# Full-height and full-width stationary operands in the mixers of a two-block network

## The chip, the cores and the metric

One NeuronCore of a Trainium2 chip runs the whole program. The metric is device time in microseconds; three runs of the kernel before took 3250.97, 3258.43 and 3259.24 us, so the median is 3258.43 us.

## The reference, cut to what matters

The input is one sequence of 512 tokens of width 1024. The first block puts 16 meta tokens in front of them (528 positions) and runs two layers, each of a SwiGLU network, a mixer and a second SwiGLU network. The second block is one layer with another mixer and a SwiGLU network. All of it is float32.

A mixer of the first block adds up two branches:

```python
# attention: 8 heads, 96 features a head for scores, 64 for values
s = einsum('bhqd,bkhd->bhqk', q, k) * 96 ** -0.5     # causal over meta and tokens
o = einsum('bhqk,bkhd->bqhd', softmax(s), v)
# recurrence: 4 heads of 128 features, decay exp(b_t - b_s) for each pair t >= s
attn = einsum('bhtk,bhtsk,bhsk->bhts', q, decay, k)
o = einsum('bhts,bhsv->bhtv', attn, v) + (what the state brings)
```

The second block's mixer has a state-space branch, and an attention branch of 8 query heads over one shared key head of 64 features, where a query sees only the 128 keys with the highest index score:

```python
rel = relu(einsum('bqhd,bsd->bqhs', qi, ki))          # 4 index heads of 64 features
iscore = einsum('bqhs,bqh->bqs', rel, wi)             # top 128 visible keys are kept
logits = einsum('bqhd,bqkd->bhqk', q, kg) * 64 ** -0.5
```

## The kernel before, in words

Activations lie with features on the partitions and positions along the free dimension, in 74 slots of 128 x 528 floats that are handed out and taken back in rotation (`alloc`, `free`, lines 262 to 275). Weights come in 512 KB chunks through three buffers on SP's DMA queue; ScalarE (ACT) and GpSimd or VectorE (POOL, DVE) split each into a high and a low part, up to four chunks ahead of their use (`split`, `ahead`). A dense product is three TensorE (PE) instructions for each 128 x 128 piece of the weight: high by high, high by low, low by high (`dense`, line 678, in the mixers; lines 400 to 402 in the networks). A product of plain float32 operands stands in the trace as two instructions, a transpose as one.

`weave` merges lists of small items by their costs into one order, so that each mixer's attention, its recurrence and the dense products of the next group of heads alternate on PE, one instruction or a few at a time. Each engine then runs its own queue in a fixed order, and engines wait for each other through semaphores.

What the change touches:

* `attention` (from line 700) serves both blocks. `s_pass` makes the scores of one head and one query block of 128 (line 719) and the exponentials. `t_pass` turns the probabilities so that keys lie on partitions: `nb` transposes of 128 x 128 (line 743), and, in the first block, one of the odd 16 keys that are left over (line 747). In the first block the keys stand with the 16 meta keys first, so that the odd keys are the last 16 tokens of the query block; only its rows from 96 on see them, and the transpose is of 32 rows and 16 columns. `o_pass` multiplies by the values: line 768 for each block of 128 keys, line 771 for the odd keys, of 16 rows and 32 columns. With one block of keys (`nb == 1`), line 768 is used twice, for query rows 0 to 95 and 96 to 127.
* `mixer`: `values` (line 954) makes the value tiles by blocks of 128 positions from position 0, the last of 16; `att_items` says which of them a head reads; `take` (line 1165) makes the products of one level of the recurrence's decay, four chunks of 128 positions each (line 1187), and for the level of 64 the quarter of each chunk that is wanted, 64 columns by 64 (line 1184).
* `block_2`: `kk_norm` (line 1569) normalizes one tile that holds the index key on partitions 0 to 63 and the key on 64 to 127, and copies it with its halves exchanged. `score` (line 1591, 4 heads for each of 3 query blocks) and `att` (line 719, 8 heads for each of 4 query blocks) take 64 partitions of the tile that has the wanted key beside the wanted head.

In the first block a layer has 8 heads and 4 query blocks of tokens, so 64 units of attention over the two layers, 16 of them with `nb == 1`; layer 0 has 8 more units for the 16 meta queries (`nb == 0`). The recurrence has 4 heads a layer and 4 chunks a head.

Of the kernel before, what the change touches and what calls it, by code (L numbers as in the profile page):

```python
# [8 lines left out]
F32 = mybir.dt.float32  # L9
# [9 lines left out]
META = 16  # L19
L = SEQ + META  # L20
# [233 lines left out]
class Kernel:  # L254
# [448 lines left out]
    def attention(self, units, geom, q, k, bias, sc, values, put):  # L703

        nc = self.nc
        U = {}

        def width(u):
            _, _, nb, meta = geom(units[u][1])
            return 128 * nb + META * meta  # L710

        def s_pass(u):
            h, qt = units[u]
            c0, n, nb, meta = geom(qt)
            qa, ka = q(h)[:, c0:c0 + n], k(h)
            w = META * meta + 128 * nb
            w0 = min(w, 512)
            ps = self.bank()
            nc.tensor.matmul(ps[:n, :w0], qa, ka[:, :w0], start=True, stop=True)
            if w > w0:  # L720
                pm = self.bank()[:n, :w - w0]
                nc.tensor.matmul(pm, qa, ka[:, w0:w], start=True, stop=True)
            p = self.alloc("p")
            nm = self.small.tile([128, 1], F32, name="nm")
            sm = self.small.tile([128, 1], F32, name="sm")
            nc.vector.tensor_tensor_reduce(p[:n, :w0], ps[:n, :w0], bias(qt)[:, :w0], -sc, 3e38, OP.add, OP.min, nm[:n])
            if w > w0:
                n0, nm = nm, self.small.tile([128, 1], F32, name="nm2")
                nc.vector.tensor_tensor_reduce(p[:n, w0:w], pm, bias(qt)[:, w0:w], -sc, n0[:n], OP.add, OP.min, nm[:n])
            self.sc.activation(p[:n, :w], p[:n, :w], AF.Exp, scale=-1.0, bias=nm[:n], accum_out=sm[:n])  # L730
            ri = self.small.tile([128, 1], F32, name="ri")
            nc.vector.reciprocal(ri[:n], sm[:n])
            U[u] = (p, ri)

        def t_pass(u):
            h, qt = units[u]
            c0, n, nb, meta = geom(qt)
            p, ri = U[u]
            ps = self.bank()
            pt = self.alloc("pt") if nb else None  # L740
            ptm = self.meta_tile("ptm") if meta else None
            for b in range(nb):
                nc.tensor.transpose(ps[:, 128 * b:128 * b + n], p[:n, 128 * b:128 * b + 128], self.ident[:n, :n])
            if meta:
                r0 = 96 if nb else 0
                pm = (ps[:META, 128 * nb:128 * nb + n - r0] if nb < 4 else self.bank()[:META, :n - r0])
                nc.tensor.transpose(pm, p[r0:n, 128 * nb:128 * nb + META], self.ident[r0:n, r0:n])

            def cp(d, s):
                if u % 2 == 0:  # L750
                    nc.vector.tensor_copy(d, s)
                else:
                    self.sc.activation(d, s, AF.Copy)
            if nb:
                cp(pt[:, :128 * nb], ps[:, :128 * nb])
            if meta:
                cp(ptm[:, :n - r0], pm)
            self.free(p)
            U[u] = (pt, ptm, ri)

        def o_pass(u):

            h, qt = units[u]
            c0, n, nb, meta = geom(qt)
            at = {}

            def times_v(b, r0, r1, start, stop):
                nc.tensor.matmul(at["bk"][r0:r1], U[u][0][:, 128 * b + r0:128 * b + r1], values(b, h), start=start, stop=stop)

            def rest(r0, start, stop):  # L770
                nc.tensor.matmul(at["bk"][r0:], U[u][1][:, :n - r0], values(nb, h)[:META], start=start, stop=stop)
            if nb == 0:
                fns = [(rest, 0, True, True)]
            elif nb == 1 and meta:
                fns = [(times_v, 0, 0, 96, True, True), (times_v, 0, 96, n, True, False), (rest, 96, False, True)]
            else:
                fns = [(times_v, b, 0, n, b == 0, b == nb - 1) for b in range(nb)]
                if meta:
                    fns.insert(1, (rest, 96, False, False))

            def fn(i, f, *args):
                if i == 0:
                    at["bk"] = self.bank()[:n, :64]
                f(*args)
                if i == len(fns) - 1:
                    pt, ptm, ri = U.pop(u)
                    nc.vector.tensor_scalar(put(h, qt)[:n, 64 * (h % 2):64 * (h % 2) + 64], at["bk"], ri[:n], None, op0=OP.mult)
                    if pt is not None:
                        self.free(pt)
            return [Item((0.00088 * width(u) + 0.1) / len(fns), lambda i=i, f=f: fn(i, *f)) for i, f in enumerate(fns)]  # L790

        n = len(units)
        items = []
        for t in range(n + 2):
            if t < n:
                items.append(Item(0.0017 * width(t) + 0.1, lambda t=t: s_pass(t)))
            if 0 <= t - 1 < n:
                items.append(Item(0.00085 * width(t - 1) + 0.1, lambda t=t: t_pass(t - 1)))
            if 0 <= t - 2:
                items += o_pass(t - 2)  # L800
        return items
# [97 lines left out]
    def mixer(self, l, st, nxt):  # L899
# [57 lines left out]
        def values():  # L957
# [1 line left out]
            hi, lo = self.split_of[f"v{l}"]  # L959
            vs = []  # L960
            for b in range(5):
                c0, nt = 128 * b, min(128, L - 128 * b)
                bk = self.bank()[:nt, :512]
                for k in range(2):
                    for i, (x, w) in enumerate(((hs, hi), (ls, hi), (hs, lo))):
                        nc.tensor.matmul(bk, x[k][:, c0:c0 + nt], w[:, k, :], start=k == 0 and i == 0, stop=k == 1 and i == 2)
                t = self.alloc(f"v{b}")
                self.sc.activation(t[:nt, :512], bk, AF.Copy)
                vs.append(t)
            S["v"] = vs  # L970
# [34 lines left out]
        def att_items(j):  # L1005
# [4 lines left out]
                return self.mask[:, 384 - 128 * qt:L] if qt < 4 else self.mask[:META, META + 384:2 * META + 384]  # L1010

            def values(b, h):
                return S["v"][b][:128 if b < 4 else META, 64 * h:64 * h + 64]

            def put(h, qt):
                if ("o", j) not in S:
# [48 lines left out]
        def hg_items(j):  # L1065
# [98 lines left out]
            def take(i):  # L1164
# [9 lines left out]
                def product(c):  # L1174
# [5 lines left out]
                        at["ps"] = self.bank()  # L1180
                    ps, (lhs, rhs) = at["ps"], X["x", i]
                    sl = slice(128 * c, 128 * c + 128)
                    if h == 64:
                        nc.tensor.matmul(ps[:64, 64 * c:64 * c + 64], lhs[:, 128 * c:128 * c + 64],
                                         rhs[:, 128 * c + 64:128 * c + 128], start=True, stop=True)
                    else:
                        nc.tensor.matmul(ps[:, nq2 * c:nq2 * c + nq2], lhs[:, sl], second(rhs[:, sl]), start=True, stop=True)
                    if c == 3:
                        keep(ps, lhs, rhs)
                        X.pop(("x", i))  # L1190
# [356 lines left out]
    def block_2(self, st, nxt):  # L1547
# [20 lines left out]

        def kk_norm():
            head_norm("kk", "kk2")  # L1570
            k2 = S["kk_"] = self.alloc("kk_")
            self.sc.activation(k2[0:64, :n], S["kk"][64:128, :n], AF.Copy)
            self.sc.activation(k2[64:128, :n], S["kk"][0:64, :n], AF.Copy)

        def vw_turn():
            e = S.pop("vw")
# [8 lines left out]

        def score(qt, h):
            w = 128 * (qt + 1)
            row = slice(64 * (h % 2), 64 * (h % 2) + 64)
            ki = S["kk" if h % 2 == 0 else "kk_"]
            ps = self.bank()[:, :w]  # L1590
            nc.tensor.matmul(ps, S[f"qi.{h // 2}"][row, 128 * qt:128 * qt + 128], ki[row, :w], start=True, stop=True)
            rel = self.alloc("rel")
            self.sc.activation(rel[:, :w], ps, AF.Relu)
            if h == 0:
# [25 lines left out]

        def att(qt):
            def q(h):
                return S[f"q.{h // 2}"][64 * (h % 2):64 * (h % 2) + 64]

            def k(h):
                return S["kk" if h % 2 else "kk_"][64 * (h % 2):64 * (h % 2) + 64]
            return self.attention([(h, qt) for h in range(8)], lambda qt: (128 * qt, 128, qt + 1, False), q, k, bias, 64 ** -0.5,
                                  lambda b, h: S["vt"][:, 68 * b:68 * b + 64], put)

        def finish():  # L1630
            for j in range(4):
                o = S.pop(("o", j))
                S["ot", j] = self.o_turn(o, None, n)
                self.free(o)
            self.free(S.pop("kk"), S.pop("kk_"), S.pop("vt"), *[S.pop(f"qi.{m}") for m in range(2)],
                      *[S.pop(f"q.{m}") for m in range(4)], *[S.pop(("sc", qt)) for qt in (1, 2, 3)])
            self.split_y(S, "yb", "ot", n)

# [168 lines left out]
        for m in range(4):  # L1807
            c += glu(m)
        P += weave(q_items, [x for qt in (1, 2, 3) for x in scores(qt)],
                   [item(lambda: load_out(0)), item(lambda: states(0), 5.0), item(lambda: load_out(1)), item(lambda: states(1), 5.0)])  # L1810
        P += weave(gates[:6 * per], [item(residual)] + tops(1) + tops(2), inner(0) + inner(1) + inner(2) + inner(3), att(0))
        P += weave(gates[6 * per:12 * per], tops(3), att(1) + att(2), c)
        P += weave(att(3) + [item(finish, 1.0)], gates[12 * per:])
# [29 lines left out]
    def setup_late(self):  # L1843
# [9 lines left out]
        nc.sync.dma_start(self.reset, self.ins["reset"])  # L1853
        self.ident = const("ident", [128, 128])
        self.halves = const("halves", [128, 128])
        self.lmask = self.cst.tile([128, len(LEVELS) + 1, 128], U8, name="lmask")
        for i in range(2):
            t = self.alloc("lm")
# [95 lines left out]
```

## Time and profile before

| what | before |
|---|---|
| median of three runs | 3258.43 us |
| the profiled execution, its own time | 3261.48 us |
| its span, first to last instruction | 3259.7 us |
| PE busy | 3174.7 us (97%), 21610 instructions |
| PE weight loads busy | 2869.4 us (88%) |
| DVE busy | 2038.7 us (63%) |
| ACT busy | 1407.6 us (43%) |
| POOL busy | 1080.1 us (33%) |
| DMA | 28.2% of 16 engines, 88 GB/s |

PE's busy time is the union of its instructions' intervals, and these overlap: a dense product of 264 columns has a duration of some 0.28 us, while the next one ends 0.12 us after it. What an instruction takes of PE's time is therefore read from ends: the end (start plus duration) of the one before, its own end, and the end of the one after. The three mixers run at about 498 to 794 us, 1742 to 2033 us and 2566 to 2800 us of the span; the rest are the networks, projections and the ends.

### The profile page before, as it was taken

To read this page: it belongs to the slowest core of one execution; us is meant where nothing else is said; L and a number is where in the kernel's file an instruction comes from. 1 tells how busy PE (TensorE), PEld (TensorE's weight loads), DVE (VectorE), ACT (ScalarE), POOL (GpSimd) and SP (SyncE) were. 2 spreads that over 40 slices of the span, in tenths; PEclk is the share of its full clock that TensorE was granted. 3 is DMA by queue.
4 is the path that set the end of the run, shared out by engine and by line. 5 is a ranking of instruction groups with operands and counts; after the bars stand their busy time and mean duration, and the time that the engine had idled before them with its cause. 6 is when DMAs were issued, how large, how long until landed. Compare 5 with 4: busy or idle time off the path is not lost. (4 is left out here: it accounts for less than half of the span.)

```text
span 3259.7 us, 53075 instructions
## 1 busy us (share of the span) xinstructions
PE 3174.7 (97%) x21610; PEld 2869.4 (88%) x21610; DVE 2038.7 (63%) x3417; ACT 1407.6 (43%) x2385; POOL 1080.1 (33%) x656
## 2 busy tenths in 40 slices
PE   9999999999999999999999999999999889999999
PEld 9999998889999999999998777888988566788988
DVE  7564456663575755856665563576757785566664
ACT  5322344444343544534544443444546335444443
POOL 3453235443222122222234453322224533322122
PEclk9999999999999999999998999999999999999999
DMA  5333221111323233233231112223235331222232
GB/s 185 124 107 106 91 87 44 46 53 59 92 72 110 83 94 104 79 97 104 89 99 54 41 52 65 85 91 104 86 103 162 105 89 56 72 91 92 91 98 97
DMA packets 106532, 289.63 MB, mean 89 GB/s; under 512 B 23088, under 2 KB 32304, under 8 KB 106288
## 3 DMA queue, kind: packets, MB, share of 16 engines
q1 hardware_dynamic: 106288, 286.24, 28.2%
q8 instruction: 170, 2.79, 0.4%
q14 instruction: 74, 0.61, 0.1%
HBM read 272.96 MB, written 13.24 MB: 88 GB/s over the span
## 5 line engine op out<-in xcount | busy, mean ns | idle before, releaser
L317 POOL TENSOR_TENSOR wlo<-raw,whi 128x1024 fp32r<-128x1024 f32 (+3 forms) x320 | 713.7, 2232 | 1488.9 <-ACT whi L218 1427.6
L218 ACT ACTIVATE whi<-raw 128x1024 fp32r<-128x1024 f32 (+2 forms) x504 | 491.5, 979 | 873.7 <-PE bank L401 329.1
L401 PE MATMUL bank<-gl,whi 128*128 128x264 f32 (+1 forms) x1408 | 439.1, 312 | 0.0
L402 PE MATMUL bank<-gh,wlo 128*128 128x264 f32 (+1 forms) x1408 | 439.1, 312 | 0.0
L400 PE MATMUL bank<-gh,whi 128*128 128x264 f32 (+1 forms) x1408 | 438.9, 312 | 0.0
L678 PE MATMUL bank<-xh,whi 128*128 128x264 f32 (+2 forms) x1224 | 428.4, 350 | 0.0
L678 PE MATMUL bank<-xl,whi 128*128 128x264 f32 (+2 forms) x1224 | 423.8, 346 | 3.0 <-DVE xl L421 2.8
L678 PE MATMUL bank<-xh,wlo 128*128 128x264 f32 (+2 forms) x1224 | 419.8, 343 | 0.0
L400 PE MATMUL bank<-xh,whi 128*128 128x264 f32 (+1 forms) x1184 | 356.5, 302 | 5.5 <-DVE t L576 4.6
L401 PE MATMUL bank<-xl,whi 128*128 128x264 f32 (+1 forms) x1184 | 355.2, 301 | 2.7 <-DVE xl L421 2.5
L402 PE MATMUL bank<-xh,wlo 128*128 128x264 f32 (+1 forms) x1184 | 355.1, 301 | 1.3 <-POOL wlo L317 1.3
L317 DVE TENSOR_TENSOR wlo<-raw,whi 128x1024 fp32r<-128x1024 f32 (+1 forms) x184 | 231.4, 1257 | 80.6 <-ACT whi L218 80.3
L400 PEld LDWEIGHTS bank<-gh,whi 128*128 128x128 f32 x1408 | 264.8, 188 | 16.0 <-issue 0.4
L402 PEld LDWEIGHTS bank<-gh,wlo 128*128 128x128 f32 x1408 | 264.9, 188 | 15.8
L401 PEld LDWEIGHTS bank<-gl,whi 128*128 128x128 f32 x1408 | 264.7, 188 | 15.7
L678 PEld LDWEIGHTS bank<-xl,whi 128*128 128x128 f32 (+1 forms) x1224 | 234.2, 191 | 28.7 <-issue 6.4
L678 PEld LDWEIGHTS bank<-xh,whi 128*128 128x128 f32 (+1 forms) x1224 | 234.4, 191 | 25.4 <-issue 6.2
L678 PEld LDWEIGHTS bank<-xh,wlo 128*128 128x128 f32 (+1 forms) x1224 | 234.1, 191 | 25.0 <-issue 8.1
L635 DVE SCALAR_TENSOR_TENSOR h<-bank,h 128x264 f32<-128x264 f32 (+1 forms) x192 | 89.6, 496 | 236.3 <-PE bank L402 235.5
L400 PEld LDWEIGHTS bank<-xh,whi 128*128 128x128 f32 x1184 | 223.1, 189 | 14.3 <-DVE t L576 5.0
L218 ACT ACTIVATE whi<-s 128x512 fp32r<-128x512 f32 x272 | 162.8, 626 | 168.1 <-PE bank L521 98.5
L401 PEld LDWEIGHTS bank<-xl,whi 128*128 128x128 f32 x1184 | 223.6, 189 | 11.3 <-DVE xl L421 3.5
(428 smaller groups left out, 7879.9 us busy)
## 6 DMA issues: line engine op xcount, KB each, us to landing
raw<-in_w_dram SPq DMA_DIRECT2D x423, 512.0 KB, 3.5
raw<-in_w_dram SPq DMA_DIRECT2D x80, 448.0 KB, 3.3
h<-in_x_dram SPq DMA_DIRECT2D x8, 264.0 KB, 5.7
s_t<-zero SPq DMA_DIRECT2D x8, 256.0 KB, 5.5
s_wo<-cm SPq DMA_DIRECT2D x16, 128.0 KB, 3.2
s_win<-cm SPq DMA_DIRECT2D x8, 256.0 KB, 2.4
s<-s_win SPq DMA_DIRECT2D x8, 256.0 KB, 4.3
s<-s_wo SPq DMA_DIRECT2D x8, 256.0 KB, 3.7
```

The source lines that it names most:

```text
L218: i = self.e.activation(out, in_, func, **kw)
L317: e.tensor_tensor(lo[:, a:b], src, hi[:, a:b].bitcast(F32), op=OP.subtract)
L400: mm(p, hi[:, wk, :m], xh[k][:, c0:c1], start=start, stop=False)
L401: mm(p, hi[:, wk, :m], xl[k][:, c0:c1], start=False, stop=False)
L402: mm(p, lo[:, wk, :m], xh[k][:, c0:c1], start=False, stop=stop)
L635: nc.vector.scalar_tensor_tensor(hv, q, alpha, hv, op0=OP.mult, op1=OP.add)
L678: self.nc.tensor.matmul(at["ps"], w[:, k0 + k, :m], xx[k][:, a:b], start=k == t == 0, stop=k == nk - 1 and t == 2)
```

## The change

Four things are made 128 by 128. In the first block's attention the keys are cut the other way round: blocks of 128 tokens, and the 16 meta keys as the odd block, which every query sees. Their probabilities are turned with a full 128 x 128 transpose, of which 16 rows are copied into one of two fixed tiles whose other 112 rows are zero; the value tile of the meta keys has zero rows too. The second block's key and index key are each copied into two tiles, one with the key on the upper 64 partitions and zeros below, one the other way round, so that the product runs over all 128 partitions of two heads' queries. The recurrence's level of 64 is computed like the other levels. The tiles for the index key and its queries are given back once the scores are made, and the room kept in each partition for descriptors of DMAs is cut to 1 KiB, since the two fixed tiles need some.

```diff
@@ t_pass
-            ptm = self.meta_tile("ptm") if meta else None
+            ptm = None
+            if meta:
+                ptm = self.padded[u % 2] if nb else self.meta_tile("ptm")
             for b in range(nb):
-                nc.tensor.transpose(ps[:, 128 * b:128 * b + n], p[:n, 128 * b:128 * b + 128], self.ident[:n, :n])
+                c = 128 * b + META * meta
+                nc.tensor.transpose(ps[:, 128 * b:128 * b + n], p[:n, c:c + 128], self.ident[:n, :n])
             if meta:
-                r0 = 96 if nb else 0
-                pm = (ps[:META, 128 * nb:128 * nb + n - r0] if nb < 4 else self.bank()[:META, :n - r0])
-                nc.tensor.transpose(pm, p[r0:n, 128 * nb:128 * nb + META], self.ident[r0:n, r0:n])
+                pm = ps[:, 128 * nb:128 * nb + n] if nb < 4 else self.bank()[:, :n]
+                m = 128 if nb else META
+                nc.tensor.transpose(pm[:m], p[:n, :m], self.ident[:n, :n])
...
-                cp(ptm[:, :n - r0], pm)
+                cp(ptm[:META, :n], pm[:META])
@@ o_pass
-            def times_v(b, r0, r1, start, stop):
-                nc.tensor.matmul(at["bk"][r0:r1], U[u][0][:, 128 * b + r0:128 * b + r1], values(b, h), start=start, stop=stop)
+            def times_v(b, start, stop):
+                nc.tensor.matmul(at["bk"], U[u][0][:, 128 * b:128 * b + n], values(b, h), start=start, stop=stop)
...
-            def rest(r0, start, stop):
-                nc.tensor.matmul(at["bk"][r0:], U[u][1][:, :n - r0], values(nb, h)[:META], start=start, stop=stop)
-            if nb == 0:
-                fns = [(rest, 0, True, True)]
-            elif nb == 1 and meta:
-                fns = [(times_v, 0, 0, 96, True, True), (times_v, 0, 96, n, True, False), (rest, 96, False, True)]
-            else:
-                fns = [(times_v, b, 0, n, b == 0, b == nb - 1) for b in range(nb)]
-                if meta:
-                    fns.insert(1, (rest, 96, False, False))
+            def rest(start, stop):
+                nc.tensor.matmul(at["bk"], U[u][1][:, :n], values(4, h)[:128 if nb else META], start=start, stop=stop)
+            fns = [(times_v, b, b == 0, b == nb - 1) for b in range(nb)]
+            if meta:
+                fns.insert(1, (rest, nb == 0, nb < 2))
+                if nb == 1:
+                    fns[0] = (times_v, 0, True, False)
@@ values
-                c0, nt = 128 * b, min(128, L - 128 * b)
+                c0, nt = (META + 128 * b, 128) if b < 4 else (0, META)
...
                 t = self.alloc(f"v{b}")
+                if b == 4:
+                    nc.gpsimd.memset(t[:, :512], 0.0)
                 self.sc.activation(t[:nt, :512], bk, AF.Copy)
@@ take, product
-                    if h == 64:
-                        nc.tensor.matmul(ps[:64, 64 * c:64 * c + 64], lhs[:, 128 * c:128 * c + 64],
-                                         rhs[:, 128 * c + 64:128 * c + 128], start=True, stop=True)
-                    else:
-                        nc.tensor.matmul(ps[:, nq2 * c:nq2 * c + nq2], lhs[:, sl], second(rhs[:, sl]), start=True, stop=True)
+                    nc.tensor.matmul(ps[:, nq2 * c:nq2 * c + nq2], lhs[:, sl], second(rhs[:, sl]), start=True, stop=True)
@@ kk_norm
-            k2 = S["kk_"] = self.alloc("kk_")
-            self.sc.activation(k2[0:64, :n], S["kk"][64:128, :n], AF.Copy)
-            self.sc.activation(k2[64:128, :n], S["kk"][0:64, :n], AF.Copy)
+            kk = S.pop("kk")
+            for key, src in (("ki", 0), ("k", 64)):
+                for i in range(2):
+                    t = S[key, i] = self.alloc(key)
+                    nc.gpsimd.memset(t[64 - 64 * i:128 - 64 * i, :n], 0.0)
+                    self.sc.activation(t[64 * i:64 * i + 64, :n], kk[src:src + 64, :n], AF.Copy)
+            self.free(kk)
@@ score
-            nc.tensor.matmul(ps, S[f"qi.{h // 2}"][row, 128 * qt:128 * qt + 128], ki[row, :w], start=True, stop=True)
+            nc.tensor.matmul(ps, S[f"qi.{h // 2}"][:, 128 * qt:128 * qt + 128], S["ki", h % 2][:, :w], start=True, stop=True)
@@ att
             def q(h):
-                return S[f"q.{h // 2}"][64 * (h % 2):64 * (h % 2) + 64]
+                return S[f"q.{h // 2}"]
             def k(h):
-                return S["kk" if h % 2 else "kk_"][64 * (h % 2):64 * (h % 2) + 64]
+                return S["k", h % 2]
@@ block_2, after the scores
+        P.append(item(lambda: self.free(S.pop(("ki", 0)), S.pop(("ki", 1)), *[S.pop(f"qi.{m}") for m in range(2)])))
@@ setup_late
+        self.padded = [self.cst.tile([128, 128], F32, name=f"padded{i}") for i in range(2)]
+        for t in self.padded:
+            nc.gpsimd.memset(t, 0.0)
@@ kernel
-    nc = bacc.Bacc("TRN2", target_bir_lowering=False, num_devices=1)
+    nc = bacc.Bacc("TRN2", target_bir_lowering=False, num_devices=1, dynamic_dma_scratch_size=1024)
```

The smaller products that stay are those of the 16 meta queries of layer 0 (`nb == 0`), the recurrence's products over 16 meta positions, the 16-column pieces of `values`, and the state-space branch's.

## Rows read from the trace of the kernel before

**Rows 1.** Busy time by stretch: mixer of layer 0, layer 1, part of it, block 2 twice.

```profile
core 0: us, PE busy (x) PEld busy (x) DVE busy (x) ACT busy (x) POOL busy (x), PEclk, DMA share, GB/s
497.60:794.00 296.40, 293.57 (x2161) 256.74 (x2161) 168.86 (x444) 128.60 (x298) 126.60 (x97) 1.00 0.15 47
1742.00:2033.00 291.00, 284.85 (x1601) 228.00 (x1601) 156.84 (x365) 125.37 (x273) 125.85 (x92) 0.95 0.16 48
1758.55:1782.44 23.89, 23.66 (x85) 18.75 (x86) 7.52 (x22) 3.89 (x11) 1.68 (x3) 0.50 0.15 45
2566.00:2629.00 63.00, 48.94 (x264) 29.73 (x263) 56.85 (x78) 24.02 (x36) 31.88 (x22) 0.86 0.22 67
2629.00:2800.00 171.00, 170.24 (x860) 126.65 (x860) 105.74 (x301) 74.67 (x132) 52.09 (x27) 1.00 0.25 73
```

**Rows 2.** PE's waits, 1742 to 2033 us: total us, times, longest us.

```profile
PE bank L1078 <- ACT kt L218: 3.4, 2, 2.3
```

**Rows 3.** PE's waits, 2566 to 2629 us: total us, times, longest us.

```profile
PE bank L440 <- ACT sq L218: 14.1, 2, 10.3
```

**Rows 4.** PE in order of time, layer 0's mixer: start, duration, instructions of one group.

```profile
518.29 0.28 PE L678 MATMUL bank<-xh,wlo 128*128 128x264 f32 x1
518.50 0.29 PE L771 MATMUL bank<-v,ptm 16*32 16x64 f32 x2
518.73 0.39 PE L678 MATMUL bank<-xh,whi 128*128 128x264 f32 x1
518.95 0.29 PE L678 MATMUL bank<-xl,whi 128*128 128x264 f32 x1
519.08 0.33 PE L768 MATMUL bank<-v,pt 128*128 128x64 f32 x2
519.22 0.37 PE L678 MATMUL bank<-xh,wlo 128*128 128x264 f32 x1
...
521.53 0.28 PE L678 MATMUL bank<-xl,whi 128*128 128x264 f32 x1
521.65 0.60 PE L743 MATMUL bank<-ident,p 128*128 128x128 f32 x4
522.18 0.19 PE L747 MATMUL bank<-ident,p 32*16 32x32 f32 x1
522.30 0.39 PE L678 MATMUL bank<-xh,wlo 128*128 128x264 f32 x1
522.53 0.28 PE L678 MATMUL bank<-xh,whi 128*128 128x264 f32 x1
522.74 0.33 PE L1184 MATMUL bank<-X 128*64 128x64 f32 x2
523.00 0.39 PE L678 MATMUL bank<-xl,whi 128*128 128x264 f32 x1
```

**Rows 5.** PE in order of time, layer 1's mixer, a unit with one key block.

```profile
1750.32 0.37 PE L678 MATMUL bank<-xh,whi 128*128 128x264 f32 x1
1750.62 0.30 PE L768 MATMUL bank<-v,pt 128*32 128x64 f32 x2
1750.85 0.39 PE L678 MATMUL bank<-xl,whi 128*128 128x264 f32 x1
```

**Rows 6.** PE in order of time, layer 1's mixer, scores over 96 partitions.

```profile
1747.04 0.28 PE L678 MATMUL bank<-xh,wlo 128*128 128x264 f32 x1
1747.16 0.84 PE L719 MATMUL bank<-k,q 96*128 96x400 f32 x2
```

**Rows 7.** PE in order of time, block 2, scores over 64 partitions.

```profile
2768.96 0.40 PE L678 MATMUL bank<-xh,whi 128*128 128x512 f32 x1
2769.29 1.12 PE L719 MATMUL bank<-kk,q 64*128 64x512 f32 x2
2770.34 0.50 PE L678 MATMUL bank<-xl,whi 128*128 128x512 f32 x1
```

**Rows 8.** POOL's zero fill of 128 x 512, grouped by line: busy us, mean ns.

```profile
L1125 POOL MEMSET A<- 128x512 f32 x8 | 4.2, 527 | 15.6 <-PE bank L722 8.3 <-PE bank L678 5.4 <-PE bank L1078 1.8
```

**Rows 9.** ACT's exchange of the key tile's halves: ns minimum, median, maximum.

```profile
L218 ACT ACTIVATE kk__2854_27105<-kk x2: 630/631/632, 2547.9 to 2548.5; 64x512 f32<-64x512 f32 x2
```

More of the change, by code (lines that the diff above doesn't have):

```diff
@@ L1012, in values @@
             def values(b, h):
-                return S["v"][b][:128 if b < 4 else META, 64 * h:64 * h + 64]
+                return S["v"][b][:, 64 * h:64 * h + 64]
             def put(h, qt):
@@ L1587, in score @@
             w = 128 * (qt + 1)
-            row = slice(64 * (h % 2), 64 * (h % 2) + 64)
-            ki = S["kk" if h % 2 == 0 else "kk_"]
             ps = self.bank()[:, :w]
-            nc.tensor.matmul(ps, S[f"qi.{h // 2}"][row, 128 * qt:128 * qt + 128], ki[row, :w], start=True, stop=True)
+            nc.tensor.matmul(ps, S[f"qi.{h // 2}"][:, 128 * qt:128 * qt + 128], S["ki", h % 2][:, :w], start=True, stop=True)
             rel = self.alloc("rel")
@@ L1634, in finish @@
                 self.free(o)
-            self.free(S.pop("kk"), S.pop("kk_"), S.pop("vt"), *[S.pop(f"qi.{m}") for m in range(2)],
+            self.free(S.pop(("k", 0)), S.pop(("k", 1)), S.pop("vt"),
                       *[S.pop(f"q.{m}") for m in range(4)], *[S.pop(("sc", qt)) for qt in (1, 2, 3)])
```

## The prediction

> **What bounds the kernel now.** I read the busy time by stretch first [rows 1]. In both mixers of the first block PE has work for nearly all of the stretch, while DVE, the next busiest, has it for little over half. The reader should see that time taken off PE there should come off the end, as long as PE isn't made to wait. In block 2 the picture changes: from 2566 to 2629 us PE has work for 49 of 63 us, and DVE for 57; from 2629 to 2800 us PE again fills the stretch.
>
> Second come PE's waits. In layer 1's mixer the longest is 2.3 us, where line 1078 waits for ACT's copy of the turned keys [rows 2]. From 2566 to 2629 us PE waits 14.1 us at line 440 for a square that hangs on DVE [rows 3]; here PE is not the bound.
>
> Third, and this carries the sum, PE's instructions in order of time, read by their ends. A dense product of 264 columns ends 0.12 us after the one before (522.81 after 522.69, and 519.24 after 519.12) [rows 4]; for 512 columns I scale that to 0.23. Whatever the next dense product ends later than this is the price of what stood between.
>
> **The change part by part.**
>
> *Odd keys times values, line 771.* The dense product before ends at 518.57, the one after at 519.12: 0.55, less 0.12, so 0.43 us [rows 4]. A pair over the whole array with the same 64 moving columns, line 768, stands just behind: 519.24 to 519.59, 0.35 less 0.12, so 0.23. Note where the small one loses: its own end comes only 0.22 after the dense product before, but the dense product behind it ends another 0.33 later, where 0.12 is normal. PE seems to empty itself when it goes from a part of the array to the whole and back. Saving 0.20 x 64 units = 12.8 us.
>
> *Odd keys turned, line 747.* Four full transposes take 0.44 us, from 521.81 to 522.25, or 0.11 each. The small one and the dense product behind it end at 522.69, another 0.44; less 0.12 it costs 0.32 [rows 4]. As a fifth full transpose it costs 0.11. Saving 0.21 x 64 = 13.4 us.
>
> *One key block.* The second of the two pieces of line 768, of 32 columns, costs 1751.24 less 1750.69 less 0.12 = 0.43 us [rows 5], and it goes; the other piece, of 96 columns, becomes a full pair, and I give it a full pair's price before and after. 0.43 x 16 = 6.9 us.
>
> *Level of 64, line 1184.* From 522.81 to 523.39, 0.58 less 0.12 = 0.46 us [rows 4]; after, a full pair with 64 moving columns, 0.23. 4 chunks x 4 heads x 2 layers = 32, x 0.23 = 7.4 us.
>
> *Block 2's attention, line 719.* From 2769.36 to 2770.84, 1.48 less 0.23 = 1.25 us for 512 keys over 64 partitions [rows 7]. What it costs over 128 the trace doesn't show. The nearest row is the first block's, over 96 partitions: 0.68 us for 400 keys (1747.32 to 1748.00) [rows 6], so 0.87 for 512. I take that, since 96 partitions are already past the half; at the other end the price could stay 1.25. The excess of 0.38 belongs to the change of tile and not to the columns, so I take it for narrower blocks too: 32 x 0.38 = 12.2 us. *The index scores, line 1591*, are of the same form: 12 x 0.38 = 4.6 us of PE's time.
>
> That is 57.3 us of PE. Now what of it reaches the end.
>
> Of the 40.5 us in the first block's mixers, PE's earlier arrival turns a part into waiting. The saving is 7% of the 587 us of the two mixers. The two waits in rows 2 and their like end on ACT, whose chain doesn't get shorter; some 15 us of PE's work ahead of such a wait would make it 1 us longer. With the eight recurrent heads each passing line 1078 and the other short waits I put the loss at 5 us (between 0 and 14, a third). That leaves 35.5.
>
> Of block 2, the 4.6 us of line 1591 fall into the stretch where PE waits for DVE anyway [rows 1, 3]: 0. Eight of the 32 products of line 719, those of the first query block, follow right behind it, with DVE still full; I count half of their 3.0 us. That leaves 10.7.
>
> *What is added.* ACT makes four copies of 64 x 512 in `kk_norm` instead of two: 1.3 us more [rows 9], in front of a weight split. The three dense projections that follow before the first score cover it, 24 x 0.23 = 5.5 us each; without that cover it costs 1.3. POOL gets four zero fills there, two for the value tiles, 0.53 each at most [rows 8], and two of 128 x 128 in the first network. POOL works for less than half of the mixers [rows 1]. The value tile's fill matters most: ACT's copy into that tile has to wait for it, POOL's queue may hold a split ahead of it, and behind the copy on ACT stand the next splits, for which POOL and then PE wait. Up to four chunks split ahead cover that. Should it show, I bound it by the ACT-caused wait of 2.3 us [rows 2] per layer, 4.6. The copies of the turned meta keys are 128 columns wide instead of 32, on ACT and DVE by turns, behind other copies; nothing. Two more slots in use while the scores run, given back sooner than before, and the cut of the DMA descriptors' room (every DMA is issued on SP's hardware queue) I put at nothing; a slot handed out too soon would be one more wait of 2.3 us. Each engine's queue is also ordered anew when the program is built: 3.4 us either way, what line 1078 waits now.
>
> Sum: 35.5 + 10.7 = 46 us. The profiled execution took 3261.5 us, so 3215 for its like; it stands 3 us above the median of the runs, against which I forecast **3212 us**.
>
> **A rule against it.** In rows 4 a small product delays its neighbours and runs beside none of them. The Trainium skill's page "TensorE: Matmul & The Clock Gate", Part 3, says the opposite for small operands: placed in different 32-row strips they run at the same time, measured 3.07 times faster for four of them, which would speak for small tiles and against zero padding. By that rule the products removed here cost nothing now and the padded ones their full price; the rows don't bear it out here.
>
> **The rivals.**
>
> *More: the clock comes back sooner.* From 1758.55 to 1782.44 us PE's granted clock is 0.50, the lower level of 1.2 GHz [rows 1]; before it PE waited the 2.3 us of rows 2, and the stretch holds four of line 1184 and three of line 747. At half clock 23.9 us lose 12. If the full-size products shorten this stretch, up to 12 us come on top, and with nothing lost in waits it is 57 + 12: 3189 us. Against it: the wait that went ahead stays, and may grow. Chance 0.13.
>
> *Less: the other engines set the pace.* If a third of the first block's 40.5 us goes into waits (27 left) and block 2 gives nothing, with the added 4.6 on the path, it is 22 us: 3236. For it: DVE's 57 of 63 us. Against: in the first block DVE, ACT and POOL have 40% or more to spare. Chance 0.13.
>
> *Slower: more stretches at half clock.* A wait of 2.3 us at line 1078 was followed by 12 us lost. All eight recurrent heads pass that line; a faster PE reaches it sooner, so the wait grows by about 1 us each. If the clock fell at five of the other seven heads, 60 us would be lost against 46 gained: 3272. It decides from four falls on. Against it: of layer 1's four heads only two wait there at all today [rows 2], and there are fewer emptyings in between. Chance 0.03.
>
> *Slower: small tiles were free.* If they ran beside their neighbours, the padded ones would add 64 x 0.11 + 64 x 0.23 + 32 x 0.23 + 32 x 0.54 (a mean of 320 keys) = 46 us: 3305. The ends in rows 4, 5 and 7 speak against it. Chance 0.01.
>
> *It isn't the tile.* If what delays the dense product behind is the change between kinds of product and not of tile, nothing changes: 3258. Against: line 768's full pair, of the same kind, doesn't delay it. Chance 0.03.
>
> **How the numbers follow.** The forecast, 36 to 57 us saved, has 0.67. The range takes it whole, most of the larger and smaller gain: 3187 to 3238. This kernel's runs can't tell less than 0.3%, some 10 us, from no change. Faster is forecast, more and less: 0.93. Same 0.03, slower 0.04.
>
> **What would show it.** Right: no form 32*16 with 32 rows, 16*32, 128*32 or 64*128 is left on PE; dense products behind lines 747, 771 and 1184 end 0.12 us after them (0.23 for 512 columns); the two mixers of the first block last some 18 us less each, and 2629 to 2800 us some 10 less, while 2566 to 2629 us stays. Wrong: PE's waits in the first block's mixers grow by more than 14 us, a pair over 128 partitions with zeros costs 1.25 us for 512 keys, or the granted clock falls at several heads.

## The result, and the profile after

Four runs of the changed kernel took 3210.53 to 3216.74 us, median 3212.63; four of the kernel before 3250.97 to 3259.24, median 3257.36. The ratio is 0.9867, 95% interval 0.9852 to 0.9883: 45 us faster, where 46 were forecast from rows and 3212 us was the number. That the sum fits does not yet mean that its terms do. The experiments below show where one of them, the gain of layer 1's mixer, rested on a stretch at half clock that other profiles of the kernel before don't have.

The page of the changed kernel, first part: busy time, share of the span, instructions.

```profile
span 3208.8 us, 53017 instructions
PE 3112.9 (97%) x21578; PEld 2871.9 (90%) x21578; DVE 2047.2 (64%) x3417; ACT 1408.8 (44%) x2387; POOL 1081.6 (34%) x664
```

The span is 50.9 us shorter. PE has 32 instructions fewer: with one key block two pieces of line 768 became one, 16 times two instructions. Its share of the span is what it was.

PE in order of time, layer 0's mixer, in the changed kernel (line 774 was 771, 746 and 750 were 743 and 747, 1185 stands for 1184 and 1187).

```profile
515.36 0.28 PE L678 MATMUL bank<-xh,wlo 128*128 128x264 f32 x1
515.48 0.33 PE L774 MATMUL bank<-v,padded 128*128 128x64 f32 x2
515.62 0.37 PE L678 MATMUL bank<-xh,whi 128*128 128x264 f32 x1
...
517.93 0.28 PE L678 MATMUL bank<-xl,whi 128*128 128x264 f32 x1
518.05 0.60 PE L746 MATMUL bank<-ident,p 128*128 128x128 f32 x4
518.49 0.27 PE L750 MATMUL bank<-ident,p 128*128 128x128 f32 x1
518.52 0.37 PE L678 MATMUL bank<-xh,wlo 128*128 128x264 f32 x1
518.72 0.28 PE L678 MATMUL bank<-xh,whi 128*128 128x264 f32 x1
518.84 0.33 PE L1185 MATMUL bank<-X 128*128 128x64 f32 x2
518.98 0.37 PE L678 MATMUL bank<-xl,whi 128*128 128x264 f32 x1
```

These answer to [rows 4], and the ends are as the prediction priced them. Line 774: 515.99 less 515.64 less 0.12 is 0.23 us, where 0.43 stood. Line 750: it ends at 518.76, 0.11 after line 746, and the dense product behind ends at 518.89, the usual 0.12 or 0.13 later. Line 1185: 519.35 less 519.00 less 0.12 is 0.23, where 0.46 stood. The forms that the prediction named, 32*16, 16*32, 128*32 and 64*128, are gone from PE's list. These aren't single lucky rows either: in layer 0's mixer the 28 products of line 771 that stand between two dense ones end them 0.54 to 0.56 us apart, and the 28 of line 774 after the change 0.33 to 0.36.

Block 2's scores over 128 partitions, half of them zeros, answer to [rows 7].

```profile
2725.20 0.39 PE L678 MATMUL bank<-xh,wlo 128*128 128x512 f32 x1
2725.43 1.02 PE L719 MATMUL bank<-k,q 128*128 128x512 f32 x2
2725.89 0.80 PE L678 MATMUL bank<-xh,whi 128*128 128x512 f32 x1
```

From 2725.59 to 2726.45 are 0.86 us, and the dense product ends 0.24 later: 0.87 was taken from the nearest row, 1.25 was the other end. The narrower blocks gained as much: between two dense products the scores of 128, 256, 384 and 512 keys took 0.85, 1.06, 1.27 and 1.48 us before and 0.45, 0.66, 0.87 and 1.09 after (medians of all such rows), so 0.39 or 0.40 less at each width.

Busy time by stretch of the changed kernel. The first two rows are a whole mixer of the first block, from the first dense product of line 678 to the last; the next two answer to the last two of [rows 1], from the first index score to the first attention product and from there to the end of the attention.

```profile
core 0: us, PE busy (x) PEld busy (x) DVE busy (x) ACT busy (x) POOL busy (x), PEclk, DMA share, GB/s
417.20:803.10 385.90, 377.57 (x2947) 356.05 (x2947) 230.51 (x527) 184.35 (x379) 174.85 (x122) 1.00 0.19 60
1647.40:2019.90 372.50, 360.36 (x2134) 312.15 (x2133) 224.44 (x436) 179.57 (x350) 169.67 (x114) 0.98 0.20 61
...
2523.90:2588.00 64.10, 43.73 (x263) 31.18 (x262) 60.24 (x88) 24.04 (x36) 31.43 (x22) 0.84 0.23 75
2588.00:2749.00 161.00, 158.07 (x856) 129.69 (x855) 100.75 (x291) 74.50 (x133) 52.44 (x28) 1.00 0.25 76
```

The same two mixers in the profile of the kernel before on which the prediction rests.

```profile
418.50:822.70 404.20, 398.71 (x2964) 358.46 (x2963) 225.25 (x527) 184.08 (x379) 171.65 (x122) 1.00 0.18 57
1667.10:2059.70 392.60, 384.92 (x2150) 313.22 (x2149) 218.26 (x436) 178.90 (x350) 170.79 (x114) 0.96 0.19 57
```

Layer 0's mixer lost 18.3 us, layer 1's 20.1, the attention of block 2 ten, and the stretch in which PE waits for DVE lost nothing (63 before, 64 after), though PE works 5 us less in it. All of that was forecast, layer 1's a little smaller. But PE's idle time grew from 5.5 to 8.3 us in layer 0's mixer and from 7.7 to 12.1 in layer 1's, and there the mean granted clock went from 0.96 to 0.98.

### The profile page after: what moved, and what is told of

It is laid out like the page before. It is cut to its first block, busy times and chain, and to the rows that moved or that the text cites. A ratio compares the mean times of both kernels' runs of the same rounds, so it can differ in the third digit from the quotient of the medians.

```text
span 3208.8 us, 53017 instructions
## 1 busy us (share of the span) xinstructions
PE 3112.9 (97%) x21578; PEld 2871.9 (90%) x21578; DVE 2047.2 (64%) x3417; ACT 1408.8 (44%) x2387; POOL 1081.6 (34%) x664
```

## The experiments

The theory: PE empties itself (it lets the products under way run out before it begins the next) when it goes between operands that fill the array and operands that fill at most half of its height or width, and each such change is paid; what PE saves comes off the end except where it then waits. The rivals: it is the clock, it is how little of the array is used, or small tiles are no loss in themselves.

**One part at a time.** The kernel before with the first block's attention changed and nothing else (all hunks of `t_pass`, `o_pass`, `values`, `setup_late` and `kernel`; the cut shows three of the lines):

```diff
+                ptm = self.padded[u % 2] if nb else self.meta_tile("ptm")
...
+                nc.tensor.transpose(pm[:m], p[:n, :m], self.ident[:n, :n])
...
+                nc.tensor.matmul(at["bk"], U[u][1][:, :n], values(4, h)[:128 if nb else META], start=start, stop=stop)
```

> The kernel before with the first block's attention part of the change alone (token blocks, meta keys as the padded odd block). Theory (each part of the array smaller than the whole costs PE an emptying): 12.8 + 13.4 + 6.9 = 33 us of PE less, some 4 us of it lost in waits, so 29 us faster (24 to 36), some 14 us in each of the two mixers of the first block, block 2 unchanged. Rival (half-clock stretches of layer 1's mixer are what the change took away): layer 1's mixer gains far more than layer 0's. Rival (the new order of the queues gains): block 2 or the networks change too.

Measured: 3226.35 us against 3257.54 (median of 16 runs), ratio 0.9906, interval 0.9892 to 0.9921: 31 us faster. By mixers:

```profile
419.40:809.00 389.60, 381.28 (x2947) 356.45 (x2946) 229.81 (x527) 184.36 (x379) 174.60 (x122) 1.00 0.19 59
1650.80:2024.00 373.20, 359.69 (x2134) 307.23 (x2133) 223.88 (x436) 180.10 (x350) 170.22 (x114) 0.99 0.19 61
```

Layer 0 gains 14.6 us, as said; layer 1 gains 19.4, more than its share of the work, with its clock at 0.99 instead of 0.96. The sum is what the theory said, but the rival that blames the clock has a point in layer 1. Block 2's mixer lasts 292.0 us as before (292.6), so the new order of the queues gained nothing there.

The recurrence's level of 64 alone:

```diff
-                    if h == 64:
-                        nc.tensor.matmul(ps[:64, 64 * c:64 * c + 64], lhs[:, 128 * c:128 * c + 64],
-                                         rhs[:, 128 * c + 64:128 * c + 128], start=True, stop=True)
-                    else:
-                        nc.tensor.matmul(ps[:, nq2 * c:nq2 * c + nq2], lhs[:, sl], second(rhs[:, sl]), start=True, stop=True)
+                    nc.tensor.matmul(ps[:, nq2 * c:nq2 * c + nq2], lhs[:, sl], second(rhs[:, sl]), start=True, stop=True)
```

> The kernel before with the recurrence's level of 64 made 128 by 128 alone. Theory: 32 x 0.23 = 7.4 us of PE less, at most 1 us of it lost: 6 to 8 us faster, half in each mixer of the first block; dense products behind the level's products end 0.12 us after them. Rival (half clock): if the 23.9 us stretch at half clock in layer 1's mixer, in which four of these products stand, is shortened by them alone, 6 to 12 us more in that mixer.

Measured: 3247.64 us, ratio 0.9968, interval 0.9958 to 0.9978: 10 us faster, 7 to 14, where 6 to 8 were expected. Layer 0's mixer lasts 400.50 us (3.7 less, half of 7.4), layer 1's 383.20 at a mean clock of 0.98: 9.4 less, of which the clock has the greater part.

Block 2's zero-padded keys alone (the hunks of `kk_norm`, `score` and `att`, and the giving back after the scores):

```diff
+                    t = S[key, i] = self.alloc(key)
+                    nc.gpsimd.memset(t[64 - 64 * i:128 - 64 * i, :n], 0.0)
+                    self.sc.activation(t[64 * i:64 * i + 64, :n], kk[src:src + 64, :n], AF.Copy)
```

> The kernel before with block 2's keys in zero-padded tiles alone. Theory: 32 x 0.38 = 12.2 us of PE less in the attention, of which 10 to 12 reach the end, and 4.6 us less in the index scores, of which none does, because PE waits for DVE there: 9 to 12 us faster, the stretch from the first score to the first attention product as long as before (63 us, give or take 2). Rival (PE sets the pace there too): 15 to 17 us faster and that stretch 4 to 5 us shorter.

Measured: 3245.37 us, ratio 0.9964, interval 0.9947 to 0.9981: 12 us faster. Block 2's mixer, from the first dense product to the last, lasts 281.40 us, exactly what it lasts in the changed kernel, against 292.60 before; the stretch of the scores lasts 64.3 us (2547.7 to 2612.0), within the 2 us allowed. So far the theory. Layer 1's mixer, which this kernel leaves alone, lasted 379.40 us, 13 less than in the first profile, at a mean clock of 1.00.

The three parts alone gain 31 + 10 + 12 = 53 us, the change 45 to 47. As far as an estimate can tell, the clock accounts for the difference. Each run on record has the granted clock averaged over its span. The 30 runs of the kernel before beside these experiments had 0.985 to 0.992 (median 0.988) and took 3265.72 to 3250.48 us; a straight line through them falls by 1.8 us for each 0.001 of clock (an estimate, the runs lie within some 2 us of it). The attention part's four runs had 0.990 to 0.992. Held against that line at their own clocks, the parts gain 26, 8 and 12 us, together 46, and the change, at 0.988 or 0.989, gains 44 in its first four runs and 45 in the next four.

**How much of it is the clock.** The kernel before once more, unchanged:

> The kernel before once more, for the clock. Rival to chance: the 23.9 us at half clock, 92 us into layer 1's mixer, stand there again. Chance, as the kernels that left that mixer alone already suggest: a stretch of another length, or none, and the mixer shorter by about half of what is missing.

Measured: 3252.87 us in its one timed run. Layer 1's mixer, and the stretch that answers to the 23.89 us at half clock of [rows 1]:

```profile
1668.60:2048.10 379.50, 371.81 (x2149) 303.08 (x2148) 219.20 (x436) 178.90 (x350) 170.97 (x114) 1.00 0.19 59
1760.10:1784.00 23.90, 23.63 (x145) 19.13 (x146) 12.78 (x38) 9.06 (x24) 4.42 (x5) 1.00 0.13 45
```

The clock did not fall at all, with the same wait at line 1078 ahead of the place (3.4 us in two waits in either profile), and PE got 145 instructions through where it had got 85. So this stretch comes and goes from run to run. The first profile has a second one in this mixer that [rows 1] don't name and the other profile doesn't have:

```profile
1823.40:1830.23 6.83, 6.83 (x27) 5.42 (x28) 3.22 (x12) 4.27 (x13) 4.53 (x3) 0.50 0.15 62
```

The 13 us between the two mixers hang on both, 30.7 us at half clock. Of the four profiles in which this mixer is as it was (this one, the first, block 2's part alone and the paired scores below), only the first shows any fall in it: the profile that the prediction read was the exception.

The changed kernel once more, unchanged:

> The changed kernel once more, for the clock. Theory (the clock's half stretches follow from waits and emptyings): in layer 1's mixer three short stretches at half clock, some 14 us together, as in the first profile. [...]

Measured: 3210.74 us, ratio 0.9861, interval 0.9843 to 0.9879. Here the mixer of layer 1 comes out nearly the same again, with three short falls, 13.7 us together as expected, in the places of the first profile:

```profile
1645.90:2016.30 370.40, 358.71 (x2133) 310.81 (x2132) 225.45 (x436) 179.56 (x350) 169.48 (x114) 0.98 0.20 61
```

The first profile of the changed kernel has a fourth, at the mixer's start:

```profile
1652.55:1655.96 3.41, 3.41 (x13) 3.00 (x13) 0.00 (x0) 2.08 (x4) 0.00 (x0) 0.50 0.33 132
1795.91:1799.32 3.41, 3.41 (x18) 3.41 (x17) 2.46 (x10) 3.41 (x13) 1.84 (x2) 0.50 0.25 100
1860.77:1864.18 3.41, 3.18 (x15) 2.94 (x15) 2.71 (x8) 1.16 (x4) 0.91 (x1) 0.50 0.28 95
```

All four come with a wait of PE: of 1.41 us at line 678, 3.31 at line 1080 (once 1078), 2.08 at line 746 and 2.43 at line 1080 again. The longest wait is the one that the faster PE runs into. The first row is PE in order of time, the second busy time in the stretch just behind it:

```profile
1740.88 0.28 PE L1080 MATMUL bank<-ident,kh 128*16 128x128 f32 x1 [3.31 <-ACT kt L218]
```

```profile
1741.30:1748.13 6.83, 6.83 (x31) 6.37 (x30) 2.27 (x7) 0.16 (x1) 1.04 (x1) 0.50 0.26 74
```

The wait was 2.3 us [rows 2]. Four stretches of 17.1 us together at half clock lose 8.5 us, the three of the second profile 6.8. So in two profiles of the changed kernel the falls stand in the same places but for one. In the kernel before they don't: the same wait of 2.3 us was followed by a fall in one profile and by none in another, and why is open.

**Take that wait away.** The changed kernel with a PSUM bank of its own for this transpose:

```diff
-                pm = self.bank() if real == 4 else ps[:, 384:512]
+                pm = self.bank()
```

> The changed kernel with a PSUM bank of its own for the recurrence's transpose of the 16 meta positions of the keys (line 1080), so that it has not to wait for ACT's copy out of the bank that it shares. Theory (this wait is what the faster PE runs into, and a half-clock stretch follows it): its 7.7 us in all go, the stretch at half clock some 92 us into layer 1's mixer goes or stays as short as 7 us, and the kernel is 5 to 12 us faster than the changed one's 3211. Rival (the wait is handed on, to line 1115, which needs what ACT copies next): waits at line 1115 grow by as much, no change within 4 us.

> The kernel with the bank of its own for line 1080 once more, on the same chip as the one above: 3204, within 4 us.

Measured: 3203.88 us (ratio 0.9840, 0.9825 to 0.9854) and, repeated, 3205.26 (0.9843, 0.9824 to 0.9863): some 7 us faster than the change alone, 5 of them at equal clock by the line above. PE's waits in layer 1's mixer, first run:

```profile
PE bank L1115 <- DVE ri L732: 3.7, 1, 3.7
PE bank L746 <- ACT p L218: 2.7, 2, 2.1
PE bank L1115 <- ACT ktm L218: 1.5, 1, 1.5
```

No wait is left at line 1080, but 5.2 us stand at line 1115, two instructions later on the same chain, where the change alone had none in this mixer: there the rival is right. The fall some 92 us into the mixer lasts 3.4 us in the first profile and is gone in the other. Yet the mixers last 382.00 and 368.40 us, 4 less each than with the change alone (385.90 and 372.50), at mean clocks of 1.00 and 0.99. In layer 0's, PE's idle time falls from 8.3 to 5.0 us. In layer 1's it stays at some 12 us, and what is gained there is the clock's: 6.8 us at half clock instead of 17.1.

**What in an operand makes it small.** The changed kernel with the meta keys' product over 96, then 64 of its partitions:

```diff
-                nc.tensor.matmul(at["bk"], U[u][1][:, :n], values(4, h)[:128 if nb else META], start=start, stop=stop)
+                nc.tensor.matmul(at["bk"], U[u][1][:96 if nb else META, :n], values(4, h)[:96 if nb else META], start=start, stop=stop)
```

> The changed kernel with the meta keys' product (line 774) over 96 of its 128 partitions. Theory: what counts is that the operand is past half the array's height, not that it is full; as line 719 of the first block, over 96 partitions, already costs no emptying, this costs what the full one costs: 0.23 us each and a time within 5 us of the changed kernel's 3211. Rival (only 128 rows are free of it): 0.4 us or more each, 64 of them: 12 us or more slower than that.

> The changed kernel with the meta keys' product over 64 of its 128 partitions. Theory: each of the 64 pays the emptying that block 2's scores over 64 partitions paid, 0.38 us on top of 0.23: 24 us of PE, 18 to 25 us slower than the changed kernel, near 3232. Rival (what costs is how little of the array is used, 16 rows by 32 columns, and half an array is cheap): less than 5 us slower.

Measured: 3210.33 us with 96 (two runs, ratio 0.9861), and 3229.05 with 64 (0.9920, 0.9904 to 0.9937), 18 us above the changed kernel. PE in order of time, first with 96 partitions, then with 64:

```profile
517.69 0.28 PE L678 MATMUL bank<-xh,wlo 128*128 128x264 f32 x1
517.81 0.33 PE L774 MATMUL bank<-v,padded 96*128 96x64 f32 x2
517.95 0.37 PE L678 MATMUL bank<-xh,whi 128*128 128x264 f32 x1
```

```profile
516.27 0.28 PE L678 MATMUL bank<-xh,wlo 128*128 128x264 f32 x1
516.48 0.43 PE L774 MATMUL bank<-v,padded 64*128 64x64 f32 x2
516.84 0.39 PE L678 MATMUL bank<-xh,whi 128*128 128x264 f32 x1
```

With 96: 518.32 less 517.97 less 0.12 is 0.23 us, as full. With 64: 517.23 less 516.55 less 0.12 is 0.56, 0.33 more; 64 of them are 21 us, of which 18 came through. That is dearer than the 16 x 32 operand of before (0.43), so the price does not go by how much of the array is unused.

The weight loads (PEld), which the text has left out so far, show what is lost. First those of line 771 and of the dense product behind it in the kernel before [rows 4], then of line 774 over 64 partitions, then over 128 in the changed kernel:

```profile
518.50 0.13 PEld L771 LDWEIGHTS bank<-v,ptm 16*32 16x32 f32 x2
518.73 0.19 PEld L678 LDWEIGHTS bank<-xh,whi 128*128 128x128 f32 x1
```

```profile
516.48 0.29 PEld L774 LDWEIGHTS bank<-v,padded 64*128 64x128 f32 x2
516.84 0.19 PEld L678 LDWEIGHTS bank<-xh,whi 128*128 128x128 f32 x1
```

```profile
515.36 0.31 PEld L774 LDWEIGHTS bank<-v,padded 128*128 128x128 f32 x2
515.59 0.19 PEld L678 LDWEIGHTS bank<-xh,whi 128*128 128x128 f32 x1
```

Between full-size operands a load begins while the products before it are well under way, 0.28 us before the end of the dense one (515.64) and 0.22 before the end of the pair (515.81). At a change of size it begins only 0.07 or 0.06 us before those ends (518.57 and 518.79, 516.55 and 516.91), together with its own product. Most of the load is then no longer hidden behind the products ahead. The pair's two loads take 0.29 us with 128 columns and 0.13 with 32, which fits that the operand of 64 x 128 is the dearer one, though no run takes the two apart.

The same with the transpose, 16 columns wide instead of 128, with all its rows:

```diff
-                m = 128 if nb else META
+                m = META
```

> The changed kernel with the meta keys' transpose (line 750) of 16 columns instead of 128, all 128 rows kept. Theory, from the recurrence's transposes of 16 columns (line 1080), behind which dense products come 0.12 us later as always: a transpose's width does not matter, 0.11 us each, a time within 5 us of 3211. Rival (width matters for a transpose as it does for the products of 64 or 32 columns): 0.3 us each, 12 us or more slower.

Measured: 3209.50 us (two runs, ratio 0.9858).

```profile
516.33 0.60 PE L746 MATMUL bank<-ident,p 128*128 128x128 f32 x4
516.76 0.27 PE L750 MATMUL bank<-ident,p 128*16 128x128 f32 x1
516.79 0.37 PE L678 MATMUL bank<-xh,wlo 128*128 128x264 f32 x1
```

The narrow transpose ends at 517.03, 0.10 after the others, and the dense product at 517.16, 0.13 later. For this transpose the change needed its 128 rows, and not its 128 columns, so for transposes the theory's word on the width is wrong. A product of 64 columns, line 1184, did pay [rows 4], and so did the piece of 32 columns of line 768 [rows 5], while its piece of 96 columns cost 0.19 us (it stands before the 1750.69 of [rows 5]; the dense product ahead of it ends at 1750.38).

**Two small tiles side by side.** The kernel before, with block 2's index scores issued for two heads at once, into two banks:

```diff
+            for h in (h0, h0 + 1):
+                row = slice(64 * (h % 2), 64 * (h % 2) + 64)
...
+                nc.tensor.matmul(ps, S[f"qi.{h // 2}"][row, 128 * qt:128 * qt + 128], ki[row, :w], start=True, stop=True)
```

> The kernel before with block 2's index scores of two heads issued one behind the other into two banks, the first over partitions 0 to 63, the second over 64 to 127. Rule of small tiles beside each other: the second runs with the first, and the two together take of PE's time what one took, 1.25 us for 512 keys (the dense product behind them ends 1.48 us after the one before). Theory (PE empties itself at a change of shape, and the tiles run one after the other): 2 x 0.87 + 0.38 = 2.1 us, and 2.5 if it empties itself between the two halves as well. No change in the time, since PE waits for DVE there.

Measured: 3253.65 us in its one timed run, no change that one run could show. PE in order of time, two heads of 512 keys:

```profile
2574.26 0.40 PE L678 MATMUL bank<-xh,wlo 128*128 128x512 f32 x1
2574.58 0.69 PE L1593 MATMUL bank<-kk,qi 64*128 64x512 f32 x1
2574.59 0.69 PE L1593 MATMUL bank<-kk__2854_27105,qi 64*128 64x512 f32 x1
2575.12 0.59 PE L1593 MATMUL bank<-kk,qi 64*128 64x512 f32 x1
2575.12 0.59 PE L1593 MATMUL bank<-kk__2854_27105,qi 64*128 64x512 f32 x1
2575.64 0.50 PE L678 MATMUL bank<-xh,whi 128*128 128x512 f32 x1
```

Here my theory missed. The two heads' products start within 0.01 us of each other, and the dense product behind ends at 2576.14, 1.48 after the one before at 2574.66: the pair costs 1.25 us, what one head alone cost [rows 7], not 2.1 or 2.5. Two halves of the array's height work at the same time when they are issued together. The Trainium skill's page "TensorE: Matmul & The Clock Gate", Part 3, says that small operands in different parts of the array run concurrently, and this run agrees: 1.25 us for two heads, against 2 x 0.86 padded. No run paired the heads of line 719, where PE sets the pace.

**A faster version.** With the bank of its own, and more of the remaining small operands padded:

```diff
-                tm = self.small.tile([META, 128], F32, name=key + "m", bufs=2)
+                tm = self.padded_m[key, j % 2]
...
-                nc.tensor.matmul(at["bk"], U[u][1][:, :n], values(4, h)[:128 if nb else META], start=start, stop=stop)
+                nc.tensor.matmul(at["bk"], U[u][1], values(4, h), start=start, stop=stop)
...
-            nc.tensor.transpose(pm[:, :META], om, self.ident[:META, :META])
+            nc.tensor.transpose(pm[:, :128], om, self.ident)
```

> The kernel with the bank of its own for line 1080, and with more of the small operands that the change left made 128 by 128, with rows of zeros: the recurrence's turned keys and values of the 16 meta positions (lines 1115 and 1225), the turn of the meta queries' output (line 816), and their product with the values (line 774 with 16 by 16). Theory, from the ends in the traces: 8 x 0.42 + 4 x 0.3 + 4 x 0.3 + 8 x 0.18 = 7 us of PE less, some 5 of it in layer 0's mixer, of which 4 to 7 reach the end: near 3198. Rival (waits of the mixers take it): no change against the kernel with the bank alone, 3204.

Measured: 3197.45 us, ratio 0.9821, interval 0.9806 to 0.9836, against 3205.26 for the bank alone on the same chip: 8 us faster, 6 of them at equal clock by the line above, within the 4 to 7 expected.

```profile
421.30:799.40 378.10, 372.50 (x2947) 355.46 (x2946) 230.50 (x527) 184.51 (x379) 174.99 (x122) 1.00 0.20 61
1640.40:2006.20 365.80, 353.70 (x2134) 306.62 (x2133) 224.62 (x436) 179.38 (x350) 169.71 (x114) 1.00 0.19 62
```

Layer 0's mixer lasts 4 us less than with the bank alone (382.00), layer 1's 2.6 to 4 less (368.40 and 369.80). There the clock may have 1.7 to 3.4 us of it, with 3.4 us at half clock against 6.8 and 10.2. This is the fastest version, 15 us under the change and 58 under the kernel before.

## Why the prediction was right

The prices. Each of the prices after was read from a row of another instruction of the right shape, and each held to 0.01 us: 0.23, 0.11, 0.23, and 0.86 for 0.87. That carried the sum. That the excess of 0.38 belongs to the change of tile was a reading from one pair of rows; block 2's rows after the change bear it out, 0.39 or 0.40 at 128 to 512 moving columns. The run over 64 partitions, with 64 moving columns and between dense products of 264 columns and not 512, gave 0.33; which of the two makes the difference is open. The run with 96 partitions showed that the full height isn't needed.

What reaches the end. Block 2 went as said: nothing of the scores' 4.6 us, because PE waits for DVE there (the stretch lasts 64 us for 63), and 10 of the 10.7 in the attention. In the first block the loss in waits was put at 5 us, between 0 and 14; PE's idle time in the two mixers grew by 2.8 and 4.4 us, 7.2 in all, inside those bounds.

What was off, and hidden by the sum. The prediction read layer 1's mixer with a stretch of 23.9 us at half clock, took it as part of the kernel before, and had no term for falls that the change brings. Against the second profile of that kernel, layer 1's mixer gained 379.5 less 372.5 = 7 us, not 18: of 20 us, 4.4 went into waits and 8.5 into four falls of the clock. Layer 0's mixer, with the clock at 1.00 in both, gained the 18.3. That the sum came out even so was partly luck. Over whole runs the kernel before has a median clock of 0.988 and the changed one 0.988 or 0.989, so the two lose about equally much to the clock; where the kernel before loses it in its usual runs, two profiles can't show. At equal clock 44 or 45 us are gained, so the saving itself isn't the clock's.

The rivals. "The clock comes back sooner" happened only against the first profile. "More stretches at half clock" is the mechanism of layer 1 in small: a longer wait, 3.3 us for 2.3, and falls in the mixer in every profile of the change, but of 3 to 7 us and not of 24, so it took back 8 of one mixer's 20 us and not all. With it came one of the prediction's own signs of being wrong, the clock falling at several heads: it did at two waits of line 1080. The other two signs didn't come. "The other engines set the pace" is true of the scores alone. "It isn't the tile" fell with the runs over 96 and 64 partitions. "Small tiles were free" was false for the kernel before, where none stood beside another, and rightly got little; its ground, that tiles can run side by side, I had dismissed as such from rows that could not show it. Nor does that ground say that a small product beside a full-size one costs nothing, as the prediction took it.

## What to carry to other kernels

Between full-size products on PE, read a small product's price from the end of the next full-size one: here it was 0.2 to 0.4 us more than that of a full-size one, and padding it with zeros to 96 or 128 rows took that off. Where two small products can be issued together in different halves, that is cheaper than padding for wide ones: 0.63 us a head against 0.86 for 512 columns. Profile the kernel before twice before counting on a stretch at half clock, and compare runs at equal mean clock before adding up the gains of parts.

## What the runs showed that was not expected

* Two products over partitions 0 to 63 and 64 to 127, issued together, started within 0.01 us and cost 1.25 us as a pair, the price of one.
* An operand of 64 x 128 cost more (0.56 us) than one of 16 x 32 (0.43), both with 64 moving columns. In both the weight load began only 0.07 us before the end of the product ahead, instead of 0.28.
* A transpose of 16 columns and 128 rows cost no emptying, while one of 32 rows and 16 columns did (0.32 us for 0.11).
* The kernel before had 23.9 us at half clock at one place in one profile and none in the next, with the same 2.3 us wait ahead of it; with a second such stretch of 6.8 us, 13 us of a mixer or 0.4% of the run.
